# Gate matrix in blocks of eight, 48 parked blocks, and one-hot columns scaled on ScalarE, in a two-layer encoder with expert retrieval

## The chip, the cores and the metric

The kernel runs on one core of a Trainium2 chip. The metric is device time in microseconds: 3034.84 us is the median of three runs (3032.85 to 3035.76). TensorE multiplies matrices, VectorE and ScalarE work on tiles element by element, GpSimd (POOL) issues the indirect gathers here and SyncE (SP) issues all other DMAs in the order of its queue.

## The reference

Two layers, each a mixer (attention over a 2-D neighbourhood in layer 0, a short gated convolution in layer 1) and then an expert retrieval; 512 tokens of 1024 features. The change touches the retrieval alone:

```
q  = (x @ w_query) as [tokens, 8 heads, 2 halves, 128]
sc = q . sub_keys                      # 128 scores per half
sv, si = top_k(sc, 16)                 # per half
cand = sv[0][:, None] + sv[1][None]    # 256 sums, the 16 best per head stay
eidx = si[0] * 128 + si[1]             # of 128 * 128 experts
g    = softmax(best)
a    = x . w_up[eidx]
out  = sum over heads and the 16 of  gelu(a) * g * w_down[eidx]
```

Every token so uses 8 x 16 = 128 of 16384 experts.

## The kernel before

The tokens stand in four chunks of 128. For chunk 3 the rows of the experts that it uses are gathered one per token with indirect DMAs (128 rows of `w_up`, 128 of `w_down`, each 128 x 1024). For the other three chunks (`TD` = 384 tokens) the experts are computed densely, in 128 key blocks of 128 experts each, and a gate matrix that is zero almost everywhere picks out what a token uses. A block has two halves:

- *up* (`dense_up`, L502): the block's 128 x 1024 weights are loaded, split into a high and a low part (L105 on ScalarE, L106 on VectorE), and 24 matmuls of 128 x 384 (L127) make `ps_up`; ScalarE turns it into `ab` by a gelu (L506). `ab` has `AHEAD + 2` = 6 buffers.
- *down* (`dense_down`, L514): VectorE multiplies `ab` by the block's gates (`w`, L527), `w` and the block's 128 x 1024 `wd` weights are split, and 18 matmuls of 128 x 512 (L543) add to six sums `acc` that stay in PSUM over all 128 blocks.

The stages of a layer's retrieval, in order:

1. Queries and keys, and the 16 best of each half (up to about 413 us in layer 0).
2. Selection (`select`, L606): gates and key indices of each token, chunk by chunk, mostly on VectorE. Nine small transposes (`ps_g`, L441) turn them, and VectorE copies them to `gT`, `iT` and `jT`.
3. One-hot stage (L446 to L468): the gate matrix is built in groups of 4 tokens. `ob` has a row of 128 for each rank of a token with a one at its first key index, `oa` the same for the second index times the gate. The product of the two (`ps_gb`, L464) is the token's gate matrix of 128 x 128. ScalarE evicts a group (L465) to `stage`, and after 32 tokens SyncE writes `stage` to `gd` in DRAM (L468). 96 groups a layer.
4. Expert stage: all 128 downs, the ups that are left, and the 256 gathers, spread evenly over them.

In a group of 4 tokens, VectorE makes the comparisons of `ob` in one instruction of 512 elements (L450), those of `oa` for the first `ACTN` = 2 tokens in one of 256 (L454), and for the other two the comparison and the multiplication by the gate in one instruction of 128 each (L462). ScalarE multiplies the first two by their gates (L460).

What TensorE does during stages 2 and 3 beside the small products are ups: `NPRE` = 52 blocks (0 to 51) are computed there, at a pace set by estimated costs (`PRE_RATE`), and their `ab` is parked in DRAM (`ad`, L508). In the expert stage they are read back two at a time (`at`, L523). The downs go in fours: 19 fours of fresh blocks (52 to 127), whose ups run up to 4 blocks ahead, and 13 of parked ones spread among them. The gate matrix is read back for one four at a time (`gt`, L518): 128 x 12 x 128 elements, in contiguous pieces of 4 x 32 elements (512 bytes). `gt` has two buffers.

The order of the instructions on each engine is made when the program is built, by a scheduler that plays the program against estimated costs; at run time each engine takes its own in that order. A line of the page is a line of the file before; in the changed file everything behind L54 stands one line lower.

Of the kernel before, what the change touches and what calls it, by code (L numbers as in the profile page):

```python
# [12 lines left out]
F32 = mybir.dt.float32  # L13
# [10 lines left out]
P = 128  # L24
# [17 lines left out]
TOPK = 16  # L42
# Pairs (r, s) of the two sorted halves that can be among the 16 largest sums: row r has
# TOPK // (r + 1) of them, in a field of a power of two.
LENS = [TOPK // (r + 1) for r in range(TOPK)]
# [4 lines left out]
TD = ND * P  # L50
NPRE = 52
PRE_RATE = 1.4
OB = 12
ACTN = 2  # L54
RING = 4
# [9 lines left out]
def encoder(ctx: ExitStack, tc: tile.TileContext, x, g_mix, g_ffn, g_ffn_row, g_fin_row, bias,  # L65
# [34 lines left out]
    def split(raw, shape, tag, name, pool=None, **kw):  # L100
        """A float32 tile as two float32r tiles whose sum it is exactly."""
        pool = pool or wpool
        hi = pool.tile(shape, F32R, name=f"{name}_h", tag=f"{tag}_h", **kw)
        lo = pool.tile(shape, F32R, name=f"{name}_l", tag=f"{tag}_l", **kw)
        nc.scalar.activation(hi, raw, AF.Copy)  # L105
        nc.vector.tensor_tensor(lo, raw, hi.bitcast(F32), op=ALU.subtract)  # L106
        return hi, lo
# [11 lines left out]
    def up_pieces(src, xh, xl, n):  # L119
        """[128 outputs, n tokens] of one column block of a matrix, in PSUM, piece by piece."""  # L120
        wh, wl = load_split(src, "wu")
        ps = ps_work("ps_up")
        k = 0
        for kc in range(KC):
            c = slice(kc * P, (kc + 1) * P)
            for a, b in ((wh, xh), (wh, xl), (wl, xh)):
                nc.tensor.matmul(ps[:, :n], a[:, c], b[:, kc, :n], start=k == 0, stop=k == 3 * KC - 1)  # L127
                k += 1
            yield ps

    def natural(t):
        """Of tokens in the order of positions: [column block, row, column of the block]."""
        return t.rearrange("p (r c w) -> p c r w", r=ROWS, w=CB)

    def chunks(t):
        """The same of tokens in the order of chunks."""
        return t.rearrange("p (c r w) -> p c r w", r=ROWS, w=CB)

    def load_root(after):
        """Has ScalarE load the root's table ahead of a norm, once a tile is there."""  # L140
        t = small.tile([P, 1], F32, name="root")
        nc.scalar.activation(t, after, AF.Sqrt, scale=0.0)

    def rstd_of(c):
        """1 / rms of a chunk's rows, a Newton step after the table's root."""
        sq = acts.tile([P, D], BF16, name="sq", tag="sq")
        v = small.tile([P, 1], F32, name="v", bufs=4)
        r = small.tile([P, 1], F32, name="r", bufs=4)
        t = small.tile([P, 1], F32, name="t", bufs=4)
        nc.scalar.activation(sq, h[:, c], AF.Square, accum_out=v)  # L150
        nc.vector.tensor_scalar(v, v, 1.0 / D, EPS, op0=ALU.mult, op1=ALU.add)
        nc.scalar.activation(t, v, AF.Sqrt)
        nc.vector.reciprocal(r, t)
        nc.vector.scalar_tensor_tensor(t, r, v, r, op0=ALU.mult, op1=ALU.mult)
        nc.vector.tensor_scalar(t, t, -0.5, 1.5, op0=ALU.mult, op1=ALU.add)
        nc.vector.tensor_mul(r, r, t)
        return r

    def norm_t(gain, name, order=range(NCH)):
        """The normed rows, transposed, as two float32r tiles [128, 8, 512]: each chunk times the  # L160
        diagonal of its 1 / rms."""
        xh = acts.tile([P, KC, S], F32R, name=f"xh{name}", tag="xh")
        xl = acts.tile([P, KC, S], F32R, name=f"xl{name}", tag="xl")
        dg = {}
        for c in order:
            r = rstd_of(c)
            dg[c] = small.tile([P, P], F32, name="dg", bufs=4)
            nc.vector.tensor_scalar(dg[c], ident, r, None, op0=ALU.mult)
        for k0 in range(0, KC, 4):
            ps = [ps_acc(f"ps_t{k}") for k in range(4)]  # L170
            for c in order:
                for k in range(4):
                    kc = k0 + k
                    nc.tensor.matmul(ps[k][:, c * P:(c + 1) * P], h[:, c, kc * P:(kc + 1) * P], dg[c],  # L174
                                     start=True, stop=True)
            for k in range(4):
                kc = k0 + k
                nc.scalar.activation(xh[:, kc], ps[k], AF.Copy, scale=gain[:, kc:kc + 1])
                nc.vector.scalar_tensor_tensor(xl[:, kc], ps[k], gain[:, kc:kc + 1], xh[:, kc].bitcast(F32),
                                               op0=ALU.mult, op1=ALU.subtract)  # L180
        return xh, xl

    def out_proj(w, yh, yl):
        """h += y @ w, y transposed and in two parts, piece by piece."""
        for half in range(2):
# [16 lines left out]

# [1 line left out]
    def attention(l):  # L204
        xh, xl = norm_t(gm[:, l], f"m{l}", (3, 0, 1, 2) if l else range(NCH))
        with tc.tile_pool(name="attn", bufs=1) as ap, tc.tile_pool(name="attn2", bufs=2) as a2:
# [3 lines left out]
            def project(m, t):  # L210
                """Queries, keys and values of two heads."""
                for n in range(3):
# [36 lines left out]
            def attend(m, t, bank):  # L249
                """Their attention; yields where TensorE has to wait."""  # L250
                kh, kl = [t[n].rearrange("p (r w) -> p r w", w=GRID_W) for n in ("kh", "kl")]
# [96 lines left out]

# [1 line left out]
    def short_conv(l):  # L350
# [27 lines left out]

# [1 line left out]
    gd = dram.tile([TD // GT, P, NK, GT], F32, name="gd")  # L380
    ad = dram.tile([NPRE // 2, P, 2, TD], F32, name="ad")

    def peer(l):
        xh, xl = norm_t(gf[:, l], f"f{l}")
        with ExitStack() as st:
# [36 lines left out]
            def retrieval():  # L422
                """Yields (DVE, PE) microseconds after each piece of it."""
                for c in (3, 0, 1, 2):
# [69 lines left out]

            # rows of w_up in fours, each four's rows of w_down after the next four's of w_up
            fours = [(gather_up, 0)]
# [18 lines left out]
            def dense_down(n, b):  # L515
                if b % 4 == 0:
                    gt = p2.tile([P, TD // GT, 4, GT], F32, name="gt")
                    nc.sync.dma_start(gt.rearrange("p g i c -> p g (i c)"),  # L518
                                      gd[:, :, b:b + 4].rearrange("g j i c -> j g (i c)"))
                    first.append(gt)  # L520
                if b < NPRE and b % 2 == 0:
# [5 lines left out]
                mark = nc.vector.tensor_tensor(w.rearrange("p (g c) -> p g c", c=GT),  # L527
                                        ab.pop(b).rearrange("p (g c) -> p g c", c=GT), gt[:, :, b % 4], op=ALU.mult)
                a_h, a_l = split(w, [P, TD], "w", "w", pool=p2)
# [32 lines left out]
            p2 = st.enter_context(tc.tile_pool(name="experts", bufs=2))  # L562
            # the downs: the blocks kept in DRAM spread evenly among the others, in fours
            fresh = list(range(NPRE // 4, NK // 4))
            kept = list(range(NPRE // 4))
            order = []
            for n, q in enumerate(fresh):
                order.append(q)
                while len(kept) and (NPRE // 4 - len(kept)) * len(fresh) <= n * (NPRE // 4):
                    order.append(kept.pop(0))  # L570
            order += kept
            blocks = [4 * q + i for q in order for i in range(4)]
            ng = done = 0
# [23 lines left out]
    def top16(s, v, i, pool, n):  # L597
        """The 16 largest of each row in order, and where they are."""
        t = pool.tile([P, n], F32, name="tk", tag=f"tk{n}", bufs=3)
# [6 lines left out]
    def select(sv, si, p2, cand):  # L606
        """Gates and the two key indices of the 16 best pairs of each head: [128, 8 * 16] each."""
        for r in range(8):
# [30 lines left out]
        def pick(which, val, table, name):  # L639
            """The key index at the rank whose step of table val is on, as a sum of differences."""  # L640
            e = big[:, 0].rearrange("p h k r -> p (h k) r")
# [48 lines left out]
def _blocks_t(w):  # L690
    """[.., 1024, n * 128] as [.., n, 128, 8 * 128]: of each block of 128 columns, by row % 128."""
    lead, n = w.shape[:-2], w.shape[-1] // P
    w = w.reshape(*lead, KC, P, n, P)
    k = len(lead)
    w = w.transpose(*range(k), k + 2, k + 1, k, k + 3)
    return np.ascontiguousarray(w).reshape(*lead, n, P, KC * P)


def _bias_tiles(rel):
    """rel_bias [16, 15, 31] as [head, query column of a block, block, key of its band]; keys  # L700
    outside a query's window get the mask's value."""
    r = np.arange(ROWS)
# [53 lines left out]
```

## Time and profile before

| what | value |
|---|---|
| median of the runs | 3034.84 us (3032.85 to 3035.76) |
| profiled execution, first to last instruction | 3030.5 us |
| TensorE busy | 2991.3 us, 99% |
| VectorE busy | 2346.7 us, 77% |
| ScalarE busy | 1362.0 us, 45% |
| DMA moved | 747.96 MB, mean 247 GB/s |
| chain that ended last | TensorE 94%, VectorE 4%, ScalarE 1% |

The profiled execution's own time is its span, 3030.5 us; a run's time is 4.3 us more at the median. The busy share of an engine is an average over the stages: ScalarE's 45% is 93% in the one-hot stage and 36% in the expert stage. "Idle before" of a group is the time its engine had nothing to do just before these instructions, with what ended it. In the text, "window" means a stretch in us from the span's start. Layer 0's one-hot stage lies at about 520 to 727 us, layer 1's at 1977 to 2183.

### The profile page before, as it was taken

Reading aid. Unit: us, or ns where it says so; the run is one execution under the profiler, and the core shown is the slowest. Engines: PE = TensorE matmul, PEld = TensorE weight load, DVE = VectorE, ACT = ScalarE, POOL = GpSimd, SP = SyncE. Lnnn points to the kernel's source line nnn. Section 1 sums busy time; section 2 is a strip of 40 time slices with the busy share of each in tenths; the row PEclk is TensorE's granted clock in tenths of the full one; section 3 lists DMA queues with packets and bytes.
Section 4 is the critical chain, followed back from the end, with each engine's and each line's share of the span. In section 5 each row is a group of like instructions: output and inputs, shape, how many; then the busy total and the mean of one; then the engine's idle time right before and its main releaser. Section 6 shows DMA issues by size and latency. Waiting matters only on the chain.

```text
span 3030.5 us, 44280 instructions
## 1 busy us (share of the span) xinstructions
PE 2991.3 (99%) x15794; PEld 2688.6 (89%) x15794; DVE 2346.7 (77%) x5131; ACT 1362.0 (45%) x2237; POOL 663.5 (22%) x571
## 2 busy tenths in 40 slices
PE   8999999999999999999999999999999999999998
PEld 7887899999888888888888888999988888888887
DVE  4444899987888888887774479998788888888786
ACT  4443236996333333333342233599833333333333
POOL 0000000001343443443410000000034434444341
PEclk9998999999999999999999999999999999999999
DMA  4322244567999999998942323556699999999995
GB/s 157 98 98 89 79 134 161 216 232 264 342 348 338 338 343 340 329 339 318 346 146 98 104 96 110 167 202 219 233 370 335 332 352 336 338 329 349 320 333 194
DMA packets 297982, 747.96 MB, mean 247 GB/s; under 512 B 23457, under 2 KB 139169, under 8 KB 294689
## 3 DMA queue, kind: packets, MB, share of 16 engines
q1 hardware_dynamic: 224032, 476.67, 45.1%
q0 software_dynamic: 73728, 268.47, 23.9%
q8 instruction: 124, 2.03, 0.3%
q14 instruction: 98, 0.79, 0.1%
HBM read 672.17 MB, written 72.88 MB: 246 GB/s over the span
## 4 chain that ended last, share of the span: by engine, by line
PE 94%; DVE 4%; ACT 1%; issue 0%; DMA 0%; DVEq 0%
PE ps_up L127 46%; PE acc L543 35%; PE ps_gb L464 6%; PE ps_o L191 3%; PE ps_t L174 1%; DVE wu_l L106 1%; PE ps_s L268 1%; PE ps_o L300 1%; PE ps_k L405 1%; PE ps_pt L287 1%; DVE tk L602 0%; ACT sq L150 0%; PE ps_v L245 0%; DVE best L600 0%; DVE pos L604 0%
## 5 line engine op out<-in xcount | busy, mean ns | idle before, releaser
L127 PE MATMUL ps_up<-xhf,wu_l 128*128 128x384 f32 (+1 forms) x2304 | 798.9, 347 | 1.1 <-DVE wu_l L106 1.1
L127 PE MATMUL ps_up<-xhf,wu_h 128*128 128x384 f32 (+1 forms) x2304 | 794.3, 345 | 2.1 <-ACT ab L506 2.0
L127 PE MATMUL ps_up<-xlf,wu_h 128*128 128x384 f32 (+1 forms) x2304 | 792.1, 344 | 0.0
L105 ACT ACTIVATE wu_h<-wu_raw 128x1024 fp32r<-128x1024 f32 x336 | 355.4, 1058 | 718.3 <-PE ps_up L127 419.5
L477 POOL DMA_INDIRECT row<-in_up,eidx x256 | 327.2, 1278 | 1310.8 <-DMA wu_raw<-in_up_t 882.3
L543 PE MATMUL acc<-wd_h,w_l 128*128 128x512 f32 x1536 | 603.5, 393 | 0.0
L543 PE MATMUL acc<-wd_l,w_h 128*128 128x512 f32 x1536 | 599.0, 390 | 0.0
L105 ACT ACTIVATE wd_h<-wd_raw 128x1024 fp32r<-128x1024 f32 x256 | 271.6, 1061 | 701.9 <-issue 616.2
L106 DVE TENSOR_TENSOR wu_l<-wu_raw,wu_h 128x1024 fp32r<-128x1024 f32 x336 | 409.7, 1220 | 184.1 <-ACT wu_h L105 182.0
L543 PE MATMUL acc<-wd_h,w_h 128*128 128x512 f32 x1536 | 514.9, 392 | 0.0
L106 DVE TENSOR_TENSOR wd_l<-wd_raw,wd_h 128x1024 fp32r<-128x1024 f32 x256 | 313.4, 1224 | 235.1 <-ACT wd_h L105 224.8
L127 PEld LDWEIGHTS ps_up<-xhf,wu_h 128*128 128x128 f32 x2304 | 433.3, 188 | 21.1 <-ACT ab L506 3.4
L127 PEld LDWEIGHTS ps_up<-xlf,wu_h 128*128 128x128 f32 x2304 | 433.0, 188 | 17.5
L127 PEld LDWEIGHTS ps_up<-xhf,wu_l 128*128 128x128 f32 x2304 | 433.1, 188 | 17.2 <-DVE wu_l L106 3.7
L477 POOL DMA_INDIRECT row<-in_down,eidx x256 | 330.6, 1291 | 509.3 <-DVE sq L484 468.3
L543 PEld LDWEIGHTS acc<-wd_l,w_h 128*128 128x128 f32 x1536 | 288.4, 188 | 61.7
L493 DVE SCALAR_TENSOR_TENSOR accg<-row,ag,accg 128x1024 f32<-128x1024 f32 x256 | 327.7, 1280 | 14.6 <-DMA row<-in_down,eidx 13.8
L543 PEld LDWEIGHTS acc<-wd_h,w_l 128*128 128x128 f32 x1536 | 288.7, 188 | 54.2
L543 PEld LDWEIGHTS acc<-wd_h,w_h 128*128 128x128 f32 x1536 | 287.2, 188 | 54.7
L484 DVE SCALAR_TENSOR_TENSOR sq<-row,hn 128x1024 bf16<-128x1024 f32 x256 | 312.2, 1220 | 3.0 <-DMA row<-in_up,eidx 1.9
L464 PE MATMUL ps_gb<-ob,oa 128*128 128x128 f32 x1536 | 209.6, 274 | 0.0
L465 ACT ACTIVATE stage<-ps_gb 128x512 f32<-128x512 f32 x192 | 204.5, 1114 | 2.0 <-PE ps_gb L464 1.3
(170 smaller groups left out, 3388.4 us busy)
## 6 DMA issues: line engine op xcount, KB each, us to landing
wd_raw<-in_down SPq DMA_DIRECT2D x256, 512.0 KB
wu_raw<-in_up_t SPq DMA_DIRECT2D x256, 512.0 KB
gd<-stage SPq DMA_DIRECT2D x24, 2048.0 KB
gt<-gd SPq DMA_DIRECT2D x64, 768.0 KB
ad<-ab SPq DMA_DIRECT2D x104, 192.0 KB
at<-ad SPq DMA_DIRECT2D x52, 384.0 KB
wu_raw<-in_w_query SPq DMA_DIRECT2D x32, 512.0 KB
wu_raw<-in_w_qkv SPq DMA_DIRECT2D x24, 512.0 KB
```

The costliest lines, as they stand in the source:

```text
L105: nc.scalar.activation(hi, raw, AF.Copy)
L106: nc.vector.tensor_tensor(lo, raw, hi.bitcast(F32), op=ALU.subtract)
L127: nc.tensor.matmul(ps[:, :n], a[:, c], b[:, kc, :n], start=k == 0, stop=k == 3 * KC - 1)
L174: nc.tensor.matmul(ps[k][:, c * P:(c + 1) * P], h[:, c, kc * P:(kc + 1) * P], dg[c], start=True, stop=True)
L191: nc.tensor.matmul(ps[c], a[:, m, c * P:(c + 1) * P], b, start=m == 0 and i == 0, stop=m == KC - 1 and i == 2)
L268: nc.tensor.matmul(ps[:, a * 256:(a + 1) * 256], q[hs, j * P:(j + 1) * P], k[hs, :, BAND0[j]:BAND0[j] + BAND], start=i == 0, stop=i == 2)
L464: nc.tensor.matmul(ps[:, n * NK:(n + 1) * NK], a, b4[:, n], start=True, stop=True)
L465: nc.scalar.activation(stage[:, :, 4 * q:4 * q + 4].rearrange("p i t -> p t i"), ps.rearrange("p (t i) -> p t i", t=4), AF.Copy)
L477: nc.gpsimd.indirect_dma_start(out=t, out_offset=None, in_=table, in_offset=bass.IndirectOffsetOnAxis(ap=eidx[:, k:k + 1], axis=0))
L484: nc.vector.scalar_tensor_tensor(o, t, 1.0, hn, op0=ALU.mult, op1=ALU.mult, accum_out=ag[:, k:k + 1])
L493: nc.vector.scalar_tensor_tensor(accg, t, ag[:, k:k + 1], accg, op0=ALU.mult, op1=ALU.add)
L543: nc.tensor.matmul(acc[c, half], aa[:, cs], ww[:, hs], start=new and i == 0, stop=n == NK - 1 and ww is held[-1][-1])
```

## The change

Three edits, in both layers:

- `ACTN` is 4: all four tokens' `oa` are compared in one instruction of 512 elements on VectorE, and all four scaled on ScalarE. The combined instruction (L462) is not reached any more.
- `GB` = 8: the gate matrix is read back for eight blocks at a time (128 x 12 x 256 elements, pieces of 1024 bytes), and the downs go in eights: ten eights of fresh blocks and six of parked ones.
- `NPRE` is 48 (a multiple of 8): four blocks fewer are computed ahead and parked; their ups come in the expert stage.

Comments and docstrings also went; they have no instructions.

```
@@ -40,18 +40,19 @@
-NPRE = 52
+NPRE = 48
 PRE_RATE = 1.4
 OB = 12
-ACTN = 2
+ACTN = 4
+GB = 8
...
@@ -513,10 +514,10 @@
             def dense_down(n, b):
-                if b % 4 == 0:
-                    gt = p2.tile([P, TD // GT, 4, GT], F32, name="gt")
+                if b % GB == 0:
+                    gt = p2.tile([P, TD // GT, GB, GT], F32, name="gt")
                     nc.sync.dma_start(gt.rearrange("p g i c -> p g (i c)"),
-                                      gd[:, :, b:b + 4].rearrange("g j i c -> j g (i c)"))
+                                      gd[:, :, b:b + GB].rearrange("g j i c -> j g (i c)"))
...
-                                        ab.pop(b).rearrange("p (g c) -> p g c", c=GT), gt[:, :, b % 4], op=ALU.mult)
+                                        ab.pop(b).rearrange("p (g c) -> p g c", c=GT), gt[:, :, b % GB], op=ALU.mult)
...
-            fresh = list(range(NPRE // 4, NK // 4))
-            kept = list(range(NPRE // 4))
+            kept = list(range(NPRE // GB))
+            fresh = list(range(NPRE // GB, NK // GB))
             order = []
             for n, q in enumerate(fresh):
                 order.append(q)
-                while len(kept) and (NPRE // 4 - len(kept)) * len(fresh) <= n * (NPRE // 4):
+                while len(kept) and (NPRE // GB - len(kept)) * len(fresh) <= n * (NPRE // GB):
                     order.append(kept.pop(0))
             order += kept
-            blocks = [4 * q + i for q in order for i in range(4)]
+            blocks = [GB * q + i for q in order for i in range(GB)]
```

The scheduler orders the instructions anew. ScalarE in the middle of the one-hot stage before (`stage` is the eviction of a group, `oa` a scaling, `wu_h` the high part of an up block's weights, `ab` its gelu):

```order
L465 ACTIVATE stage<-ps_gb 128x4x128 x2
L460 ACTIVATE oa<-oa,gT 128x128 x4
L465 ACTIVATE stage<-ps_gb 128x4x128
L105 ACTIVATE wu_h<-wu_raw 128x1024
L460 ACTIVATE oa<-oa,gT 128x128 x2
L506 ACTIVATE ab<-ps_up 128x384
```

The same place in the changed kernel, one whole turn of a pattern that repeats:

```order
L466 ACTIVATE stage<-ps_gb 128x4x128
L106 ACTIVATE wu_h<-wu_raw 128x1024
L507 ACTIVATE ab<-ps_up 128x384
L461 ACTIVATE oa<-oa,gT 128x128 x4
L466 ACTIVATE stage<-ps_gb 128x4x128 x2
L461 ACTIVATE oa<-oa,gT 128x128 x8
```

A turn has three groups (3 evictions, 12 scalings) and one block's split and gelu; before, about seven groups went with two blocks.

TensorE at the end of layer 0's one-hot stage before (`ps_gb` are the one-hot products, `ps_up` the ups; the numbers are those of tiles that have several):

```order
L464 MATMUL ps_gb<-ob,oa 128x128 x4
L127 MATMUL ps_up<-xhf_2609,wu_h 128x384
L127 MATMUL ps_up<-xlf_2610,wu_h 128x384
L127 MATMUL ps_up<-xhf_2609,wu_l 128x384
...
L127 MATMUL ps_up<-xlf_2610,wu_h 128x384
L543 MATMUL acc_7535<-wd_h,w_h 128x512
```

95 up matmuls stand there between the last one-hot product and the first product of the expert stage (`acc`). The same place in the changed kernel:

```order
L128 MATMUL ps_up<-xlf_2610,wu_h 128x384
L128 MATMUL ps_up<-xhf_2609,wu_l 128x384
L465 MATMUL ps_gb<-ob,oa 128x128 x24
L544 MATMUL acc_7399<-wd_h,w_h 128x512
L544 MATMUL acc_7403<-wd_h,w_h 128x512
```

The last six groups' products stand in one piece, and the expert stage's first product right behind them. Counted over TensorE's order from the last key scores on, 624 up matmuls of 128 x 384 stand ahead of the first one-hot product before and 578 now, 675 and 766 between the first and the last one, and 95 and none ahead of the first `acc`.

## Rows read from the trace of the kernel before

**Rows 1.** the page: TensorE's busy time; GB/s in 40 slices of the span

```profile
span 3030.5 us, 44280 instructions
...
PE 2991.3 (99%) x15794; PEld 2688.6 (89%) x15794; DVE 2346.7 (77%) x5131; ACT 1362.0 (45%) x2237; POOL 663.5 (22%) x571
...
GB/s 157 98 98 89 79 134 161 216 232 264 342 348 338 338 343 340 329 339 318 346 146 98 104 96 110 167 202 219 233 370 335 332 352 336 338 329 349 320 333 194
```

**Rows 2.** stretch, length, busy PE, PEld, DVE, ACT, POOL; clock, DMA share, GB/s

```profile
560.00:720.00 160.00, 160.00 (x1140) 160.00 (x1139) 139.97 (x330) 149.38 (x274) 0.00 (x0) 1.00 0.62 229
740.00:1540.00 800.00, 800.00 (x3895) 708.71 (x3895) 654.90 (x856) 287.63 (x421) 325.67 (x253) 1.00 0.94 338
420.00:520.00 100.00, 98.44 (x561) 96.23 (x560) 99.25 (x437) 58.71 (x70) 0.00 (x0) 1.00 0.50 166
```

**Rows 3.** TensorE's groups, 560-720 us: count, busy us, mean ns, idle

```profile
L464 PE MATMUL ps_gb<-ob,oa 128*128 128x128 f32 x615 | 84.1, 274 | 0.0
L127 PE MATMUL ps_up<-xhf,wu_l 128*128 128x384 f32 x175 | 63.1, 360 | 0.0
```

**Rows 4.** TensorE's timeline at 720 us: start, length, what

```profile
720.32 1.05 PE L464 MATMUL ps_gb<-ob,oa 128*128 128x128 f32 x8
721.13 0.42 PE L127 MATMUL ps_up<-xhf,wu_l 128*128 128x384 f32 x1
721.39 0.34 PE L127 MATMUL ps_up<-xhf,wu_h 128*128 128x384 f32 x1
721.57 0.34 PE L127 MATMUL ps_up<-xlf,wu_h 128*128 128x384 f32 x1
```

**Rows 5.** ScalarE's groups, 560 to 720 us

```profile
L465 ACT ACTIVATE stage<-ps_gb 128x512 f32<-128x512 f32 x77 | 81.9, 1113 | 0.4 <-PE ps_gb L464 0.2
L460 ACT ACTIVATE oa<-oa,gT 128x128 f32<-128x128 f32 x153 | 52.2, 391 | 10.3 <-DVE oa L454 10.2
L105 ACT ACTIVATE wu_h<-wu_raw 128x1024 fp32r<-128x1024 f32 x22 | 23.1, 1051 | 0.1
L506 ACT ACTIVATE ab<-ps_up 128x384 f32<-128x384 f32 x22 | 10.9, 496 | 0.0
```

**Rows 6.** ScalarE's timeline, first scalings and first evictions of layer 0

```profile
496.00 1.27 ACT L460 ACTIVATE oa<-oa,gT 128x128 f32<-128x128 f32 x4
497.49 0.70 ACT L460 ACTIVATE oa<-oa,gT 128x128 f32<-128x128 f32 x2 [0.22 <-DVE oa L454]
...
524.50 2.08 ACT L465 ACTIVATE stage<-ps_gb 128x512 f32<-128x512 f32 x2
```

**Rows 7.** VectorE's groups, 560 to 720 us

```profile
L450 DVE TENSOR_TENSOR ob<-iota,iT 128x512 f32<-128x512 f32 x77 | 52.9, 687 | 12.1 <-PE ps_gb L464 10.7
L462 DVE TENSOR_SCALAR oa<-iota,jT,gT 128x128 f32<-128x128 f32 x154 | 46.0, 341 | 0.0
L454 DVE TENSOR_TENSOR oa<-iota,jT 128x256 f32<-128x256 f32 x77 | 32.2, 418 | 0.0
```

**Rows 8.** timeline of ScalarE, SyncE, VectorE, TensorE, 725 to 742 us

```profile
725.47 1.13 ACT L465 ACTIVATE stage<-ps_gb 128x512 f32<-128x512 f32 x1
...
726.63 0.33 SPq L468 DMA_DIRECT2D gd<-stage  x1
...
733.75 0.38 SPq L518 DMA_DIRECT2D gt<-gd  x1
...
739.98 0.56 DVE L527 TENSOR_TENSOR w<-ab,gt 128x384 f32<-128x384 f32 x1 [4.56 <-DMA gt<-gd]
...
741.74 1.54 PE L543 MATMUL acc<-wd_h,w_h 128*128 128x512 f32 x6
```

**Rows 9.** the chain of waits, 724 to 750 us: start, us, what

```profile
725.43 16.47 PE ps_up L127 x95
```

**Rows 10.** busy us by stretch ahead of layer 0's second norm

```profile
295.00:300.00 5.00, 1.54 (x7) 1.54 (x8) 4.08 (x23) 4.82 (x13) 0.02 (x1) 0.82 0.71 239
300.00:305.00 5.00, 5.00 (x40) 5.00 (x40) 2.58 (x11) 0.97 (x2) 0.00 (x0) 0.84 0.00 0
```

## Prediction

> **What bounds the kernel now.** I read the page's first section, then the busy times by stretch, then each engine's groups inside the one-hot stage, then the timeline at the handover to the expert stage. TensorE is busy for 2991 of 3030.5 us [rows 1], but "busy" can hide waiting, because matmuls overlap, so I check it stage by stage. In the selection (420 to 520 us of layer 0) TensorE has 98.4 of 100 us and VectorE 99.3; in the one-hot stage (560 to 720) TensorE has all 160, ScalarE 149.4, VectorE 140.0; in the expert stage (740 to 1540) TensorE has all 800 and the DMA engines stand at 0.94 [rows 2]. So ScalarE has 10.6 us in 160 to spare where the change works, and TensorE none.
>
> Is the one-hot stage truly TensorE's? It holds 615 of the one-hot products (two instructions a product, eight a group of 4 tokens: 77 groups) and three times 175 up matmuls [rows 3]. A group takes 0.81 us (720.32 to 721.13), the up matmul behind it 0.26, an ordinary one 0.174 (721.39 to 721.57) [rows 4]. So 77 x (0.81 + 0.09) + 525 x 0.174 = 160.7 us against the 160 that passed: TensorE does not wait, and a group costs 160 / 77 = 2.08 us because some 6.8 up matmuls go with it.
>
> **ScalarE's part of the one-hot stage.** It makes 77 evictions, 153 scalings, 22 high parts of up weights and 22 gelus [rows 5]. The change doubles the scalings: 4 a group, not 2. Four in a row take 1.27 us, two take 0.70 [rows 6], so one more costs (1.27 - 0.70) / 2 = 0.285 us; the group's own figure, 52.2 / 153 = 0.34 us [rows 5], is the upper end. The lower end is 0.24 us, what 128 elements cost with nothing fixed: an eviction of 512 takes 81.9 / 77 = 1.06 us [rows 5], so 384 elements more cost 0.72. I take 0.29, since the scalings will stand four and eight in a row. In the new order of ScalarE three groups go with one weight split and one gelu, so 77 groups bring 25.7 of those and not 22. Sum for 77 groups: 149.4 + 154 x 0.29 + 3.7 x (1.05 + 0.50, less 0.2 of overlap) = 149.4 + 44.7 + 5.0 = 199 us, or 2.59 us a group. TensorE's need in that order is 0.90 + 8 x 0.174 = 2.29 us a group. ScalarE becomes the bound by 0.3 us a group, and 0.5 above today's pace.
>
> **VectorE's part.** Per 77 groups it loses 46.0 + 32.2 us of narrow compares and gains another set like the first operand's, 52.9 us [rows 7]: 25 us less, 0.33 a group. VectorE is not what the stage waits for, so I cost this gain at nothing; the ends are 0 and the whole of it, the rival below.
>
> **How long the one-hot stage gets, per layer.** Before, its first eviction starts at 524.5 and its last ends at 726.6 [rows 6, 8]: 202 us for 96 groups. In the new order of TensorE the first product stands behind 578 up matmuls of this phase instead of 624, so 46 x 0.174 = 8 us sooner, at 516.5; until the last selection is through, VectorE feeds it at about the same pace as ScalarE can take. 96 x 2.59 = 248.6 us, so the last eviction ends near 765, 38 us later. With the bounds of a scaling (0.24 and 0.34) this is 28 to 48.
>
> **The handover, per layer.** Now 95 up matmuls stand between the last product and the first expert product: 16.5 us [rows 9], which hide the gate matrix's way through memory. It goes: last eviction ends at 726.6, write issued 726.6, read issued 733.8, first gated block at 740.0, first expert product 741.7 [rows 8], so 15.1 us from the eviction. In the new order the 24 last one-hot instructions of the program are followed at once by the first expert product: by then TensorE has done 1344 up matmuls (56 blocks, 48 parked and the 8 that buffers allow), and nothing is left to hide those 15 us. SyncE issues the same sequence (write, two reads of the gate matrix, two parked blocks), but each read is 1.57 MB instead of 0.79. Of the 6.2 us from read to use that adds between nothing and another 6.2; I take 2, the time of 0.79 MB more at 370 GB/s, the best of the page's slices [rows 1]. So the first expert product comes at 765 + 15.1 + 2 = 782, 40.4 us later than 741.7. TensorE also has less behind it then: 1344 up matmuls against 624 + 675 + 95 = 1394, and 50 x 0.174 = 8.7 us of work are still to do in the full expert stage.
>
> After such a wait TensorE starts slowly: a wait ahead of the norm's transposes, 3.5 us of it in the first of two windows of 5 us, shows a granted clock of 0.82 and 0.84 in them [rows 10], part of the time at the lower level of 1.2 GHz. That is 0.34 x 5 = 1.7 us of lost clock in both windows, some of it while idle. For a wait of 17 us I take 2.5 (0 to 6).
>
> Sum: 40.4 + 8.7 + 2.5 = 51.6 us a layer, 103.2 for two, which I take alike.
>
> **The 48 parked blocks and the runs of eight.** Four blocks a layer move from the one-hot stage to the expert stage; TensorE's work in all is the same, and the 8.7 us above already carry what that changes at the stage's start. The expert stage's order gets runs of 8 parked blocks, whose products need more loads per matmul. TensorE does not wait there now in 800 us at a DMA share of 0.94 [rows 2]; up matmuls of coming blocks are mixed into the parked runs, and the gate matrix comes in half as many pieces. I take 0; the bounds are -2 and +20 us a layer. A gate read that waits for its buffer holds SyncE's later weight loads, but its buffer is free after the eighth block, two or more blocks before the loads behind it are due.
>
> **A page's price for the scaling.** The rows show a scaling of 128 elements at 0.34 us of engine time, and 0.285 more for each one that follows in a row [rows 5, 6]. The Trainium skill, "ScalarE: Activation LUTs", section "Rules for kernel authors", budgets about 0.3 us for an activation and 0.83 ns an element, which would be 0.41 us (an estimate from that page) and bring 2.82 us a group and 3183 us in all; the trace measures less, so the rows decide. The same table says to leave multiplications to VectorE, against what the change does.
>
> **Rivals.**
> 1. *ScalarE just fits (13%).* If scalings and evictions run closer together than the rows, TensorE keeps its pace of 2.29 us: 516.5 + 96 x 2.29 = 736, the first expert product at 753, so 11.7 + 8.7 + 2.5 = 22.9 us a layer: 3081. It decides at (2.29 x 3 less the 3 evictions and one block, about 4.1) / 12 = 0.23 us a scaling. No row shows one so short.
> 2. *The clock falls (7%).* TensorE will wait about 0.9 us in each cycle of 7.8. If that brings the lower level for stretches as that wait did, a stretch of 20 us needs 6.9 x 2 = 13.7 us a cycle and loses 8.6; two a layer give 3138 + 4 x 8.6 = 3172. Against: the stretch keeps 88% of its work. "TensorE: Matmul & The Clock Gate", section "Loop structure matters more than you think" in the Trainium skill, warns of waits between matmuls; it names long ones, and by it this rival would not come.
> 3. *The expert stage starts to wait (8%).* Runs of eight parked blocks outrun the loads at a DMA share of 0.94: 20 us a layer more, 3178.
> 4. *Not slower (5%).* VectorE, not TensorE, sets the pace of the one-hot stage, and the 0.33 us a group are gained: 96 x 0.33 x 2 = 63 us, 2972. For it: ScalarE's scalings sat idle 10.3 us for compares [rows 5]. Against: the sum of 160.7 in 160 us above, and ScalarE's 199 us for what had to fit in 160. It decides only if ScalarE's group stays under 1.75 us, less than its work today (149.4 / 77 = 1.94). The most that TensorE's idle time offers is 1.6 us a layer [rows 2], which would be no change (2% of the 5).
>
> **How the numbers follow.** The profiled execution spans 3030.5 us; the median of three runs is 3034.8, 4.3 above it. 3030.5 + 103.2 + 4.3 = 3138 us, with 67% for this case. Its own range, from a scaling of 0.24 to 0.34 us, a read of +0 to +6 and the clock, is 3110 to 3172. Down to rival 1 and up to rivals 2 and 3, the range is 3095 to 3180. A change under 0.2% (6 us) can't be told from none. Faster 3%, same 2%, slower 95%.
>
> **What would show it.** Right: ScalarE busy over 95% in the one-hot stage, 96 evictions in about 249 us, TensorE idle before its one-hot products on ScalarE's scalings, a gap of 14 to 20 us ahead of the first expert product with no up matmuls in it, and an expert stage of 1.00 TensorE again. Wrong: TensorE still at 100% there, up matmuls in the handover, or idle TensorE past the first 20 us of the expert stage.

## The result and the profile after

The changed kernel takes 3126.86 us at the median of four runs (3125.17 to 3128.43), the kernel before 3033.85 beside it: 93.0 us longer, a ratio of 1.0311 [1.0299, 1.0323]. The forecast was 3138, its range 3095 to 3180. The profiled execution of the changed kernel spans 3123.4 us, 92.9 more than that of before [rows 1].

The page of the changed kernel, from its first section (span; busy us of each engine, share of the span, instructions) and its chain that ended last:

```profile
span 3123.4 us, 44277 instructions
...
PE 3030.5 (97%) x15794; PEld 2708.5 (87%) x15794; DVE 2297.2 (74%) x4747; ACT 1455.6 (47%) x2621; POOL 667.8 (21%) x571
...
DMA packets 246588, 744.80 MB, mean 238 GB/s; under 512 B 22752, under 2 KB 88288, under 8 KB 243296
...
PE 79%; ACT 13%; DVE 5%; issue 2%; DMA 1%; DVEq 0%; ACTq 0%; SPq 0%
```

TensorE has the same 15794 matmuls as before, ScalarE 384 instructions more and VectorE 384 fewer. ScalarE's busy share over the whole span, 47%, still looks harmless, but 13% of the chain is now its own; before it was 1%. Which stages pay is seen stage by stage (start:end and length, then busy us of PE, PEld, DVE, ACT, POOL, then the granted clock, the DMA share and GB/s), layer 0:

```profile
560.00:720.00 160.00, 156.23 (x1026) 149.53 (x1026) 101.66 (x148) 160.00 (x364) 0.00 (x0) 1.00 0.54 197
740.00:760.00 20.00, 15.98 (x91) 14.52 (x90) 9.97 (x15) 19.79 (x44) 0.00 (x0) 0.83 0.43 159
760.00:780.00 20.00, 2.44 (x6) 1.96 (x7) 2.37 (x5) 1.80 (x4) 3.90 (x4) 0.53 0.88 320
780.00:800.00 20.00, 20.00 (x93) 17.38 (x92) 16.03 (x25) 5.96 (x9) 9.39 (x7) 0.96 0.91 322
800.00:1580.00 780.00, 780.00 (x3810) 692.58 (x3809) 636.57 (x825) 280.15 (x409) 316.24 (x245) 1.00 0.92 331
```

Against [rows 2]: in the one-hot stage ScalarE has gone from 149.4 to all 160 us, and TensorE does 1026 matmuls there instead of 1140. Its busy time fell by only 3.8 us, the waits that its one-hot products show there:

```profile
L465 PE MATMUL ps_gb<-ob,oa 128*128 128x128 f32 x514 | 81.3, 287 | 3.8 <-ACT oa L461 3.8
```

By the prices of [rows 4], 64.25 groups at 0.90 us and 512 up matmuls at 0.174 are 147 us of work, so 13 of the 160 us were lost and only 3.8 show as idle. The count of matmuls tells more here than the busy share. The window 760 to 780 is nearly empty of TensorE work. Past 800 us it is full again.

Two of ScalarE's groups and VectorE's three in 560 to 720 us (count, busy us, mean ns of one, idle time before):

```profile
L461 ACT ACTIVATE oa<-oa,gT 128x128 f32<-128x128 f32 x256 | 93.3, 737 | 0.0
L466 ACT ACTIVATE stage<-ps_gb 128x512 f32<-128x512 f32 x64 | 81.2, 1453 | 0.0
```

```profile
L455 DVE TENSOR_TENSOR oa<-iota,jT 128x512 f32<-128x512 f32 x64 | 43.7, 683 | 0.0
L451 DVE TENSOR_TENSOR ob<-iota,iT 128x512 f32<-128x512 f32 x63 | 43.0, 683 | 0.0
L107 DVE TENSOR_TENSOR wu_l<-wu_raw,wu_h 128x1024 fp32r<-128x1024 f32 x21 | 25.7, 1225 | 56.1 <-ACT wu_h L106 56.1
```

64 groups pass in 160 us where 77 did [rows 5], so a group takes 2.50 us and not 2.08. ScalarE is never idle. VectorE's compares are cheaper, 0.68 + 0.68 us a group against 1.70 [rows 7], but it now waits 56.1 us for ScalarE's high parts: its gain is idle time. One turn of ScalarE's pattern, on its timeline (start, length, what):

```profile
599.05 1.24 ACT L106 ACTIVATE wu_h<-wu_raw 128x1024 fp32r<-128x1024 f32 x1
600.01 0.64 ACT L507 ACTIVATE ab<-ps_up 128x384 f32<-128x384 f32 x1
600.38 1.44 ACT L461 ACTIVATE oa<-oa,gT 128x128 f32<-128x128 f32 x4
601.55 2.21 ACT L466 ACTIVATE stage<-ps_gb 128x512 f32<-128x512 f32 x2
603.39 2.57 ACT L461 ACTIVATE oa<-oa,gT 128x128 f32<-128x128 f32 x8
605.69 1.24 ACT L466 ACTIVATE stage<-ps_gb 128x512 f32<-128x512 f32 x1
606.54 1.25 ACT L106 ACTIVATE wu_h<-wu_raw 128x1024 fp32r<-128x1024 f32 x1
```

From 599.05 to 606.54 is 7.49 us for three groups, 2.50 a group. Read from start to start, twelve scalings take 1.17 + 2.30 = 3.47 us (0.289 each), three evictions 2.69 (0.90 each), the split 0.96 and the gelu 0.37. The lengths overlap and would sum to more.

TensorE's waits in layer 0, 515 to 1600 us (what waited for what: us in all, times, longest), and its timeline at the handover:

```profile
PE acc L544 <- ACT w_h L106: 18.9, 1, 18.9
PE ps_gb L465 <- ACT oa L461: 6.9, 26, 1.6
```

```profile
754.67 3.93 PE L465 MATMUL ps_gb<-ob,oa 128*128 128x128 f32 x18
777.55 2.93 PE L544 MATMUL acc<-wd_h,w_h 128*128 128x512 f32 x6 [18.95 <-ACT w_h L106]
780.28 0.52 PE L128 MATMUL ps_up<-xhf,wu_h 128*128 128x384 f32 x1
780.60 0.52 PE L128 MATMUL ps_up<-xlf,wu_h 128*128 128x384 f32 x1
...
781.54 0.33 PE L128 MATMUL ps_up<-xlf,wu_h 128*128 128x384 f32 x1
781.71 0.34 PE L128 MATMUL ps_up<-xhf,wu_l 128*128 128x384 f32 x1
```

No up matmul stands between the last one-hot product and the first expert product any more. The wait is charged to ScalarE's `w_h`, but the chain of waits names what lies behind it (start, us, what):

```profile
758.01 1.79 ACT stage L466 x2
759.80 0.02 issue
759.82 6.29 DMA gd<-stage
...
766.24 9.88 DMA gt<-gd
...
776.34 0.57 DVE w L528
```

The gate matrix's way through memory, write and read, is in the open.

### The profile page after: what moved, and what is told of

It reads as the page before. It is cut to its first block, busy times and chain, and to the rows that moved or that the text cites. A ratio compares the mean times of both kernels' runs of the same rounds, so it can differ in the third digit from the quotient of the medians.

```text
span 3123.4 us, 44277 instructions
## 1 busy us (share of the span) xinstructions
PE 3030.5 (97%) x15794; PEld 2708.5 (87%) x15794; DVE 2297.2 (74%) x4747; ACT 1455.6 (47%) x2621; POOL 667.8 (21%) x571
## 2 busy tenths in 40 slices
DMA packets 246588, 744.80 MB, mean 238 GB/s; under 512 B 22752, under 2 KB 88288, under 8 KB 243296
## 4 chain that ended last, share of the span: by engine, by line
PE 79%; ACT 13%; DVE 5%; issue 2%; DMA 1%; DVEq 0%; ACTq 0%; SPq 0%
PE ps_up L128 37%; PE acc L544 34%; ACT oa L461 7%; ACT stage L466 4%; PE ps_o L192 3%; ACT wu_h L106 2%; PE ps_t L175 1%; DVE wu_l L107 1%; PE ps_o L301 1%; PE ps_s L269 1%; PE ps_k L406 1%; DMA gt<-gd 1%; ACT ab L507 1%; PE ps_pt L288 1%; PE ps_gb L465 0%
## 5 line engine op out<-in xcount | busy, mean ns | idle before, releaser
L128 PE MATMUL ps_up<-xhf,wu_h 128*128 128x384 f32 (+1 forms) x2304 | 800.3, 347 | 2.1 <-ACT ab L507 2.0
L106 ACT ACTIVATE wu_h<-wu_raw 128x1024 fp32r<-128x1024 f32 x336 | 374.7, 1115 | 689.9 <-PE ps_up L128 365.0
L544 PE MATMUL acc<-wd_h,w_h 128*128 128x512 f32 x1536 | 503.8, 394 | 38.7 <-ACT w_h L106 38.7
L461 ACT ACTIVATE oa<-oa,gT 128x128 f32<-128x128 f32 x768 | 275.3, 691 | 4.6 <-DVE oa L455 4.6
L465 PE MATMUL ps_gb<-ob,oa 128*128 128x128 f32 x1536 | 242.5, 290 | 13.7 <-ACT oa L461 13.7
```

The source lines that it names most:

```text
L461: nc.scalar.activation(a, a, AF.Copy, scale=gT[:, t:t + 1])
L465: nc.tensor.matmul(ps[:, n * NK:(n + 1) * NK], a, b4[:, n], start=True, stop=True)
L544: nc.tensor.matmul(acc[c, half], aa[:, cs], ww[:, hs], start=new and i == 0, stop=n == NK - 1 and ww is held[-1][-1])
```

## The experiments

All are the changed kernel with the edits shown, except two that are the kernel before with one edit (`a_actn4`, `f_npre48`). All compute the whole result. The runs were made on several chips, on which the kernel before took 3032.3 to 3033.9 us; a difference of two kernels' medians below can hold up to 1.5 us that are the chip's. The table gives each median with its ratio to the kernel before on the same chip, and for layer 0 of its trace the end of the last eviction, the start of the first expert product, the length of the expert stage from there to the end of its last product, and the up matmuls that stand before the one-hot products, among them, and between them and the first expert product.

| kernel | us | ratio | last eviction | first expert product | expert stage | ups |
|---|---|---|---|---|---|---|
| before | 3033.85 | 1 | 726.6 | 741.7 | 821.0 | 624 / 675 / 95 |
| after | 3126.86 | 1.0311 [1.0299, 1.0323] | 759.8 | 777.6 | 831.7 | 578 / 766 / 0 |
| a_actn4 | 3090.21 | 1.0188 [1.0171, 1.0205] | 762.3 | 776.1 | 815.8 | 578 / 808 / 54 |
| f_npre48 | 3053.50 | 1.0069 [1.0055, 1.0082] | 726.7 | 741.6 | 831.7 | 624 / 675 / 45 |
| b_actn2 | 3065.76 | 1.0108 [1.0091, 1.0125] | 727.3 | 746.8 | 831.6 | 624 / 675 / 45 |
| m_actn3 | 3073.40 | 1.0135 [1.0119, 1.0150] | 731.5 | 750.7 | 831.3 | 600 / 725 / 19 |
| d_evict2 | 3092.41 | 1.0196 [1.0179, 1.0213] | 742.5 | 760.1 | 831.4 | 578 / 766 / 0 |
| l_split | 3113.54 | 1.0265 [1.0251, 1.0279] | 759.1 | 771.9 | 832.3 | 578 / 766 / 0 |
| c_ahead8 | 3115.10 | 1.0266 [1.0249, 1.0284] | 761.8 | 781.2 | 817.2 | 578 / 808 / 54 |
| h_actn4_56 | 3079.71 | 1.0152 [1.0136, 1.0167] | 762.2 | 780.5 | 802.1 | 578 / 808 / 118 |
| g_actn2_56 | 3046.60 | 1.0046 [1.0033, 1.0060] | 726.5 | 748.6 | 821.6 | 624 / 675 / 119 |
| n_all | 3046.09 | 1.0041 [1.0027, 1.0055] | 748.9 | 764.7 | 800.3 | 578 / 837 / 99 |

### The wide compare alone

```
-ACTN = 2
+ACTN = 4
```

Edit on the kernel before.

> The kernel before with all four scalings on ScalarE (ACTN 4), reads of the gate matrix in fours and 52 parked blocks as before. Theory (ScalarE paces the one-hot stage, and what is left uncovered in the handover comes on top): the stage's last eviction near 762 as in the changed kernel, but 54 up matmuls (9 us) stand in the handover, first expert product at 777 with 46 up matmuls more done than before: 35 - 8 = 27 us a layer and some clock, 3090 us. Rival (the scalings are the whole cost, blocks and reads are free): 3127. Rival (the reads of eight and the runs of eight parked blocks cost it): 3034.

3090.21 us, 57.9 above before, as expected. Its one-hot stage is the changed kernel's (length, busy PE, PEld, DVE, ACT):

```profile
560.00:720.00 160.00, 156.26 (x1026) 149.55 (x1026) 101.62 (x148) 160.00 (x363) 0.00 (x0) 1.00 0.54 201
```

So the slower pace comes with this edit alone. Its 52 parked blocks leave 54 ups behind the one-hot products, so TensorE waits 6.6 us at the handover and not 18.9.

### The changed kernel with two scalings a group

```
-ACTN = 4
+ACTN = 2
```

> The changed kernel with two scalings a group on ScalarE again (ACTN 2); 48 parked blocks and reads of eight stay. Theory: the one-hot stage runs at TensorE's 2.1 us a group again (last eviction near 727), only 45 of 95 up matmuls are left to cover the handover, first expert product at 744 with 50 up matmuls fewer done: 2.7 + 8.7 + 1 of clock = 12 us a layer, 3059 us. Rival (the scalings are the whole cost): 3034. Rival (reads and runs of eight are the cost): 3127.

3065.76 us, 61.1 below the changed kernel. TensorE is back at 1140 matmuls in the 160 us and the last eviction at 727.3. I had expected 3059. What remains, 33.4 us above before on the same chip, lies in the handover and the expert stage.

### 48 parked blocks alone

```
-NPRE = 52
+NPRE = 48
```

Edit on the kernel before.

> The kernel before with 48 parked blocks and nothing else changed (reads and runs of four, two scalings on ScalarE). Theory (parked blocks are the cover of the handover): 45 up matmuls in place of 95 ahead of the first expert product, which still comes at 741.5 since the gate matrix's way sets it; 8.7 us of ups are done later, and the wait of 7 us lowers the clock a little: 10 us a layer, 3053 us. Against the kernel with reads of eight (3066 measured) this leaves 12 us for the longer first read. Rival (48 parked blocks are free, and the reads of eight cost all of the 31 us of that kernel): 3034.

3053.50 us, 20.0 above before, as expected. The first expert product comes when it did, 741.6 against 741.7: the way through memory sets that, not TensorE. But TensorE has 50 ups less behind it by then and waits instead, and the expert stage is 10.7 us longer. From this kernel to `b_actn2` only the reads and runs of eight are added: 33.4 - 20.0 = 13.4 us. The later first expert product carries nearly all of it: in layer 0 it comes at 746.8 and not 741.6, in layer 1 21.5 us behind the last eviction and not 14.1. The three parts, 57.9 + 20.0 + 13.4 = 91.3 us, make all but 2 of the 93.0.

### Three scalings a group

```
-ACTN = 4
+ACTN = 3
```

> The changed kernel with three of four scalings on ScalarE (ACTN 3); 48 parked blocks, reads of eight. Theory (a threshold: only what ScalarE has over TensorE's pace costs): ScalarE's turn of three groups and one block is 9 x 0.292 + 2.67 + 1.33 = 6.6 us, just under TensorE's 6.9, so the stage runs at TensorE's pace with last eviction near 733, first expert product 18 us later at 752, ups done 1344 as in the changed kernel: 21 us a layer, 3076 us, 10 over the kernel with two scalings (3066) and 50 under that with four. Rival (each scaling moved costs the same): halfway, 3096.

3073.40 us, near the 3076 expected: 7.6 above two scalings and 53.5 below four. The cost is not linear; it has a threshold between three and four. The stage at 560 to 720 us, and ScalarE's two largest groups and TensorE's one-hot products in it:

```profile
560.00:720.00 160.00, 160.00 (x1134) 160.00 (x1133) 128.32 (x247) 160.00 (x346) 0.00 (x0) 1.00 0.60 220
```

```profile
L466 ACT ACTIVATE stage<-ps_gb 128x512 f32<-128x512 f32 x75 | 85.5, 1178 | 0.0
L461 ACT ACTIVATE oa<-oa,gT 128x128 f32<-128x128 f32 x227 | 76.9, 464 | 0.0
L465 PE MATMUL ps_gb<-ob,oa 128*128 128x128 f32 x595 | 83.6, 274 | 0.0
```

ScalarE shows 160.00 of 160 us here too, and yet TensorE does 1134 matmuls and does not wait for a scaling once. Both engines are full: by the turn's prices ScalarE's 75 evictions, 227 scalings and 22 blocks need 162 us, and by those of [rows 4] TensorE's 595 one-hot products and 539 ups need 161. Three scalings are about the edge. ScalarE's busy share of 100% did not tell this kernel from the one with four; TensorE's count of matmuls and its waits did. The 7.6 us are TensorE's order: 19 ups and not 45 are left for the handover, where it waits 17.1 us in layer 0 and not 12.9: 4.2 more there, against 3.8 a layer.

### Every second eviction on VectorE

```
-  nc.scalar.activation(so, pi, AF.Copy)
+  if q % 2:
+      nc.vector.tensor_copy(so, pi)
+  else:
+      nc.scalar.activation(so, pi, AF.Copy)
```

> The changed kernel with every second group of one-hot products evicted by VectorE, not ScalarE. Theory (ScalarE paces the stage): ScalarE's turn of three groups falls from 7.5 to 6.2 us, under TensorE's 6.9; 2.29 us a group, last eviction near 736, wait ahead of the expert stage as in the changed kernel: 23 us a layer over the kernel before, 3080 us. Rival (TensorE's many switches between one-hot and up matmuls, or the chain compare, scale, multiply, set the pace, not ScalarE's load): 3127. Rival (VectorE is filled by it): slower than 3127.

3092.41 us, 34.5 below the changed kernel. The two engines now share the work:

```profile
560.00:720.00 160.00, 160.00 (x1115) 160.00 (x1115) 143.89 (x195) 144.94 (x358) 0.00 (x0) 1.00 0.59 217
```

The scalings were left as they are; taking other work off ScalarE gave the pace back: the last eviction ends 17.3 us sooner in layer 0. It was ScalarE's sum, not the scalings as such or the wide compare. I had expected 3080, 12 us less: a group takes (742.54 - 517.75) / 96 = 2.34 us, TensorE's own need in this order (2.29 by the forecast), not before's 2.08, because eight up matmuls still go with each group.

### The read of eight as two reads of four

```
-  nc.sync.dma_start(gt..., gd[:, :, b:b + GB]...)
+  for i in range(0, GB, 4):
+      nc.sync.dma_start(gt[:, :, i:i + 4]..., gd[:, :, b + i:b + i + 4]...)
```

> The changed kernel with each read of eight blocks of the gate matrix issued as two reads of four into the halves of the same tile. Theory (the first product waits for a first read twice as long, 17.8 and 18.5 us after the last eviction and not 15.1): the first gated block can start when the first half is there: 3 us a layer less, 3121 us. Rival (what takes longer is all the traffic that is issued there at once, so the half lands no sooner): 3127.

3113.54 us: 13.3 below the changed kernel, where half as much was expected. SyncE's and VectorE's timelines at the handover (of the split kernel; `gd` write, `gt` read, first gated block):

```profile
759.09 0.33 SPq L469 DMA_DIRECT2D gd<-stage  x1
765.51 6.90 SPq L520 DMA_DIRECT2D gt<-gd  x4
...
770.68 0.56 DVE L529 TENSOR_TENSOR w<-ab,gt 128x384 f32<-128x384 f32 x1 [17.70 <-DMA gt<-gd]
```

From issue to the first gated block it is 770.68 - 765.51 = 5.2 us; in the changed kernel 776.34 - 766.24 = 10.1, before 6.2 [rows 8]. The first block needs only the first half. The write and the issue lie as in the changed kernel (6.4 us apart), so the cost was the size of what is read as one piece, not its place in the queue. Before's read of the same size took 6.2 us in layer 0 and 4.9 in layer 1, those of `a_actn4` 5.2 and 6.7, so the first half came as a read of four does.

### Up matmuls eight blocks ahead

```
-AHEAD = 4
+AHEAD = 8
```

> The changed kernel with 10 buffers for the gelus' results instead of 6 (AHEAD 8), so that ups run four blocks further ahead; ScalarE's work in the one-hot stage nearly the same. Theory (the wait ahead of the first expert product is paid in full): 96 more up matmuls (16.7 us) are done by the first expert product, 54 of them in the wait, at 2.3 us more of ScalarE, and the clock falls less: 14 to 16 us a layer less, 3097 us. Rival (the wait is given back later, since the expert stage catches up or then waits for loads): 3127.

3115.10 us; I had expected 18 less. In layer 0 the shorter expert stage (817.2) repays the four blocks as I thought, and it ends 10.9 us sooner than in the changed kernel. Layer 1 by itself is 3.0 us longer. TensorE's waits there, 2000 to 3100 us:

```profile
PE acc L544 <- ACT w_h L106: 22.4, 4, 17.4
PE ps_gb L465 <- ACT oa L461: 4.7, 26, 0.2
PE acc L544 <- DVE w_l L107: 3.0, 2, 2.1
```

17.4 us are the handover. Ahead of the end, 3040 to 3080 us, the same query gives 4.9 and 3.0 us on `w_h` and `w_l`: waits that the changed kernel doesn't have. They fit with ups done early that are missing later, between the last runs of parked blocks; that reading was not tested by itself.

### 56 parked blocks

```
-NPRE = 48
+NPRE = 56
```

> The changed kernel with 56 parked blocks, all else as changed (four scalings on ScalarE). Theory (ScalarE's stage stays at 2.5 us a group, but the wait in the handover is covered by 118 up matmuls): last eviction at 762, first expert product at 781 with 110 up matmuls more done than before: 39 - 19 = 20 us a layer, 3074 us, so half of the change's loss stays with ScalarE. Rival (more ups load ScalarE further and the gain is given back): 3110 or more.

3079.71 us, 47.2 below the changed kernel, near what was expected. 118 ups stand behind the last one-hot product; TensorE doesn't wait at the handover in layer 0 and waits 3.5 us in layer 1, and layer 0's expert stage is 29.6 us shorter. The one-hot stage is as slow as ever.

### Two scalings and 56 parked blocks

```
-NPRE = 48
+NPRE = 56
-ACTN = 4
+ACTN = 2
```

> The changed kernel with two scalings on ScalarE and 56 parked blocks, reads and runs of eight. Theory (reads and runs of eight cost nothing but the wait ahead of the first expert product, and 119 up matmuls, 20.7 us, now cover its 19.5 us): first expert product at 746.5 with 24 up matmuls more done than before: 5.0 - 4.2 = 1 us a layer, 3035 us. Rival (runs of eight starve TensorE in the expert stage, or the eight-block reads delay weight loads): 3050 or more.

3046.60 us, a miss by 11. With the pace and the cover both restored I had no reason left for a loss. SyncE's timeline of this kernel shows a part of one:

```profile
726.49 0.32 SPq L469 DMA_DIRECT2D gd<-stage  x1
730.31 0.32 SPq L509 DMA_DIRECT2D ad<-ab  x1
731.19 0.70 SPq L112 DMA_DIRECT2D wu_raw<-in_up_t  x1
735.07 0.38 SPq L519 DMA_DIRECT2D gt<-gd  x1
```

What the read's issue waited for, from SyncE's waits at 720 to 775 us (us, times, longest):

```profile
SPq L519 <- DMA gd<-stage: 3.1, 1, 3.1
```

The read is issued 8.6 us after the write and not 7.4 as in `b_actn2`. A parked store and a weight load stand between the two, but SyncE is done with them at 731.9 and then waits 3.1 us for the write to land. So the write takes longer; why was not tested. The read of eight is long as well: the first expert product comes 22.1 us behind the last eviction, 2 later than expected. Another part lies near the end of the expert stage, where TensorE waits 2.2 us in layer 0 and 1.8 in layer 1. ScalarE's `w_h` waits there for VectorE's gated block (layer 0, 1500 to 1572 us):

```profile
ACT w_h L106 <- DVE w L528: 5.0, 5, 3.2
```

Runs of eight alone don't bring this: `b_actn2` and the changed kernel have them and show no such wait. The four kernels that show it, in one layer or both (`c_ahead8`, `h_actn4_56`, `g_actn2_56`, `n_all`), have runs of eight and more ups done ahead. No run had 56 parked blocks in fours, so which of the two it takes is open, and so is the rest of the 11 us.

### Everything that helped together

Evictions shared as in `d_evict2`, the read split as in `l_split`, `NPRE` = 56; four scalings kept.

> The changed kernel with all four scalings kept on ScalarE and three repairs: every second group evicted by VectorE, the reads of eight issued as two of four, 56 parked blocks. Theory (ScalarE's pace, the gate matrix's way and the missing cover are all there is): one-hot products end near 750, the gate matrix is there 13 us after the last eviction and 99 up matmuls (17 us) cover that, first expert product at 769 with 120 up matmuls more done than before (21 us): 7 us a layer, and some 3 for VectorE's late rows in the last run of eight, 3052 us. Rival (something else in the new order costs, such as TensorE's switches between one-hot and up matmuls): 3075 or more. Faster than before would need TensorE to do less work, which none of these does.

3046.09 us, where 3052 was expected, 80.8 below the changed kernel and still 13.6 above before on the same chip (3032.45). TensorE waits neither for scalings nor at the handover in layer 0. What the rest is, I did not settle. Its trace spans 10.0 us more than before's: layer 0 ends 2.3 us later, the wait ahead of layer 1's first norm is 4.5 us and not 1.4, and 2.2 us are waits of layer 1's expert products, of which before shows none. No version beat the kernel before; before's TensorE shows no wait in these stages and none of these edits takes work off it, so they had nothing to win there.

## Why the prediction was right, step by step

**The bound.** The claim that TensorE sets before's one-hot stage and ScalarE has 10.6 us in 160 to spare held: two scalings (`b_actn2`) keep TensorE full, three still fit, four don't, and work taken off ScalarE (`d_evict2`) gives the pace back.

**ScalarE's pace.** Forecast 2.59 us a group, measured 2.50; 96 groups took 241.6 us (518.24 to 759.80), forecast 248.6. The scaling was right (0.29 taken, 0.289 measured). What was mis-sized is the base of the sum, the 149.4 us busy before. Priced from start to start, as in the turn above, before's 77 groups need 77 x 0.90 + 153 x 0.289 + 22 x (0.96 + 0.37) = 142.8 us; the other 6.6 were slack inside busy time. 142.8 + 154 x 0.289 + 3.7 x 1.33 = 192.2 us, 2.50 a group. 96 groups at that are 239.6 us, 9.0 less than forecast; 7.0 are seen, and the first eviction came 1.7 later than forecast, so the last one ended at 759.8 and not 765.

**VectorE's gain at nothing.** Right: it saves 0.34 us a group (0.33 forecast), and spends them waiting.

**The handover.** Forecast 15.1 + 2 us from the last eviction to the first expert product, measured 777.55 - 759.80 = 17.75. That is a near hit of two misses: the read's extra was 3.9 (10.1 against 6.2) and not 2, the other steps took 1.2 less. 3.9 lies inside the bounds of 0 to 6.2 that the text gave, twice what the fastest of the page's slices gave; a read that everything waits for did not run at that rate. In layer 1 both misses are larger: the read took 2279.16 - 2268.25 = 10.9 us against 2196.42 - 2191.51 = 4.9 before, close to the upper bound, the other steps 2.6 less, and the whole 18.5 against 15.1. That no up matmul would be left to hide it held, and `h_actn4_56` shows that 118 of them hide it, but for 3.5 us in layer 1.

**50 ups and the clock.** Forecast 8.7 + 2.5, measured 831.7 - 821.0 = 10.7: the ups' 8.7 and some 2.0 for the clock. The granted clock stands at 0.53 in 760 to 780 us and 0.96 after; the up matmuls start 0.32 us apart until 781.54 and 0.17 from there on, against 0.174 [rows 4], so TensorE had its lower level for the first 4 us of new work. `f_npre48` shows the same 10.7 with nothing else changed in the pace.

**The expert stage at nothing else.** Right in the changed kernel: 780.00 of 780 us at a DMA share of 0.92. The 51,394 packets fewer (246,588 against 297,982) bought nothing there. In `g_actn2_56` the expert stage has waits of some 2 us a layer near its end, inside the bounds of -2 to +20.

**The sum.** 35.8 + 10.7 = 46.5 us in layer 0 (51.6 forecast), 46.2 in layer 1: 92.9 by the two spans, 103.2 forecast. The difference of some 5 us a layer is nearly all the base of ScalarE's sum (7.0 us in layer 0, less 1.7 for the later first eviction).

**The rivals.** ScalarE just fits: falls at four scalings, since TensorE waits for them; at three it is what happens (`m_actn3`), with ScalarE just full. The clock falls in the one-hot stage: no, the window 560 to 720 has 1.00; only at the last six groups, which stand without ups between them, does 740 to 760 fall to 0.83. The expert stage starts to wait: not in this kernel. Not slower: falls with the pace.

## What to carry to other kernels

Before work is moved to an engine that looks half idle, sum its work in the one stage that the work goes to, priced from start to start of back-to-back instructions, and set it against the pace of the engine that bounds the stage: here one scaling more a group cost 7.6 us, the next 53.5. A count that sets work ahead (blocks parked, runs read at once) also decides what hides a way through memory; list what stands in that gap in the new order. Where only the first piece of a read is waited for, issue that piece by itself.

## What the runs showed of the hardware

ScalarE's mean length of one scaling went from 391 ns [rows 5] to 464 with three scalings and 737 with four, while the distance between starts stayed near 0.29 us: with the engine always supplied, the recorded lengths overlap, and their mean is not a price. Nor does a busy share of 100% tell an engine that is just full (three) from one that holds the others up (four).

From the issue of a stage's first read of the gate matrix to the first block that used it, a read of four blocks (0.79 MB) took 4.9 to 6.7 us in both layers of five kernels, the split reads of `l_split` and `n_all` among them, and a read of eight (1.57 MB) 9.7 to 13.2 in the other seven. The block waited for the whole read, though it used an eighth of it or a quarter.

With some eight up matmuls between the groups, waits of 3.8 us spread over 160 left the granted clock at 1.00; one wait of 18.95 us left it at the lower level for the first 4 us of work behind it.
